# Row sums of a 16384 x 1024 matrix: 200 columns of the last row loaded by two loads over 104 and 24 partitions

## The chip, the cores and the metric

The kernel runs on one core of a Trainium2 chip. The metric is the device time of one execution in microseconds (us); smaller is better. A profile is one execution recorded by the hardware profiler.

## The reference

The input `x` has shape 32 x 512 x 1024 in float32 (67.1 MB), the output 32 x 512. Each output is the sum of 1024 numbers:

```
def reference(x):
    return np.sum(x, axis=-1).astype(np.float32)
```

There is one addition for each number read, so the work is mostly the reading of 67 MB.

## The kernel before

The 32 x 512 = 16384 rows are laid out as 8 groups of 128 partitions x 16 rows (`BIG` = 16): partition p of group g holds 16 consecutive rows, and every row is 4 KB. All loads are issued by SP (SyncE) on one DMA queue, so they are worked off in the order in which they are issued. Sums collect in one tile `sums` of 128 x 128.

The order of the loads is written out by hand. First come 7 rows per partition of the last group (`FIRST` = 7, a load that is moved to the program's entry). Then come the seven other groups whole, 16 rows per partition each, in tiles `t` with three buffers. The rest of the last group follows: six rows, two rows, and at last one row, row 15 of each partition. That last row comes in two pieces of columns, `pieces = (536, 488)`: the first piece is the load at L222, the second the load at L223. L180 issues all the loads before. Each load has 128 partitions.

Sums are made in three ways. `vec` (L141) is a reduction on DVE (VectorE) over up to 16 rows. `halves` (L155) is an operation on DVE that adds the two halves of a row and accumulates the sum; it is followed by a read of the accumulator. `act` (L168) is an activation on ACT (ScalarE) with an accumulator. The last whole group and the rows behind it are split between `halves` on DVE and `act` on ACT.

For the last row, `halves` first works on the first piece (268 pairs of numbers) and writes the sum into a column of the tile right ahead of the second piece. A zero stands behind the second piece (a memset at L220), which makes it 490 numbers. The second call of `halves` (245 pairs) sums this, so the first piece's sum is added in along the way. Its result goes to the last column of `sums`.

Two stores (L191) write the output: one on ACT's queue with the first seven groups (56 KB), which is held until the load of two rows has landed and waits for the sums, and one on SP's queue with the last group (8 KB) behind the last `halves`. At the program's end the clearing of the semaphores on POOL waits for this store.

Of the kernel before, what the change touches and what calls it, by code (L numbers as in the profile page):

```python
# [101 lines left out]
def kernel(  # L102
# [5 lines left out]
    nc = tc.nc  # L108
# [14 lines left out]
    def rows_from(j, n):  # L123
        return x_g[j // BIG, :, j % BIG : j % BIG + n, :]
# [3 lines left out]
    last = J // BIG - 1  # L128
    FIRST = 7
    pieces = (536, 488)  # L130

    with (
        tc.tile_pool(name="in", bufs=3) as inpool,
        tc.tile_pool(name="unread", bufs=4, space=bass.MemoryType.PSUM) as upool,
        tc.tile_pool(name="stage", bufs=1) as stpool,
        tc.manual_schedule(),
    ):
        sums = stpool.tile([P, J], fp32)

        def vec(dst, src):  # L140
            return nc.vector.tensor_reduce(  # L141
                out=dst, in_=src, axis=mybir.AxisListType.X, op=mybir.AluOpType.add
            )

        def hold(inst, until, reason):
            tc.add_manual_dep(
                inst.ins,
                until.ins.name,
                mybir.DependencyInfo(mybir.DependencyClass.Sync, mybir.DependencyReason.DATA),
                reason=reason,  # L150
            )

        def halves(dst, src):
            n = src.shape[-1] // 2
            return nc.vector.tensor_tensor_reduce(  # L155
                out=src[:, :n],
                in0=src[:, :n],
                in1=src[:, n:],
                scale=1.0,
                scalar=0.0,  # L160
                op0=mybir.AluOpType.add,
                op1=mybir.AluOpType.add,
                accum_out=dst,
            )

        def act(dst, src, n):
            unread = upool.tile([P, dim], fp32)
            nc.scalar.activation(  # L168
                out=unread[:, :n],
                in_=src,  # L170
                func=mybir.ActivationFunctionType.Copy,
                accum_out=dst,
            )

        sums_of = []

        def rows(t, a, n, j, n_act, pairs=False):
            nv = n - n_act
            block = t[:, a * dim : (a + n) * dim].rearrange("p (n d) -> p n d", d=dim)
            load = nc.sync.dma_start(out=block, in_=rows_from(j, n))  # L180
            if pairs:
                for q in range(nv):
                    sums_of.append(halves(sums[:, j + q : j + q + 1], block[:, q, :]))
            else:
                sums_of.append(vec(sums[:, j : j + nv], block[:, :nv, :]))
            for q in range(nv, n):
                act(sums[:, j + q : j + q + 1], block[:, q, :], dim)
            return load

        def store(eng, g0, g1):  # L190
            return eng.dma_start(  # L191
                out=out_v[:, g0:g1],
                in_=sums[:, g0 * BIG : g1 * BIG].rearrange("p (g j) -> p g j", j=BIG),
            )


        j = last * BIG
        t = inpool.tile([P, BIG * dim + 4], fp32)
        rows(t, 0, FIRST, j, 0)
        first = sums_of[-1]  # L200
        for g in range(last):
            t = inpool.tile([P, BIG * dim + 4], fp32)
            if g < last - 1:
                load = rows(t, 0, BIG, g * BIG, 0)
            else:
                rows(t, 0, BIG, g * BIG, 7, pairs=True)
            if g == 1:
                hold(load, first, "no descriptors of later loads while the first ones start")

        t = inpool.tile([P, BIG * dim + 4], fp32)  # L210
        rows(t, FIRST, 6, j + FIRST, 2, pairs=True)
        two = rows(t, FIRST + 6, 2, j + FIRST + 6, 1, pairs=True)
        a = BIG - 1

        j += a
        c, width = pieces
        whole = t[:, a * dim + c : BIG * dim + 2]
        nc.vector.memset(whole[:, width + 1 :], 0.0)  # L220
        part = t[:, a * dim : a * dim + c]
        nc.sync.dma_start(out=part, in_=rows_from(j, 1)[:, 0, :c])  # L222
        nc.sync.dma_start(out=whole[:, 1 : width + 1], in_=rows_from(j, 1)[:, 0, c:])  # L223
        hold(store(nc.scalar, 0, last), two, "its packets come behind those of the loads")
        halves(whole[:, :1], part)
        halves(sums[:, j : j + 1], whole)
        store(nc.sync, last, last + 1)
# [30 lines left out]
```

## Time and profile before

| What | us |
|---|---|
| median of three runs | 161.61 |
| the three runs | 161.74, 161.48, 161.61 |
| span of the profiled execution | 160.3 |
| the profiled execution's own time | not among the times shown |
| DVE busy | 120.6 (75% of the span) |
| ACT busy | 11.9 (7%) |
| HBM read | 67.11 MB, with writes 419 GB/s over the span |
| SP issues the load at L222, at L223 | at 126.15, at 126.65 |
| these loads, from issue to landing | 31.4 each |
| last store on SP, from issue to landing | 1.4 |

The span runs from the first to the last recorded instruction; the run's time has some work around it besides. "Landing" is the moment at which a load's semaphore has its last increment; a load that is split over 16 DMA engines gets 16 of them, each from a small closing packet on one engine. Instructions named DVEq or SPq are on the sequencer of the engine, which handles waits and DMA issues. A DMA share of 1.00 in a stretch means that on average all 16 DMA engines were busy; it can read a little over 1, since records of neighbouring packets overlap.

### The profile page before, as it was taken

To read this page: it belongs to the slowest core of one execution; us is meant where nothing else is said; L and a number is where in the kernel's file an instruction comes from. 1 tells how busy PE (TensorE), PEld (TensorE's weight loads), DVE (VectorE), ACT (ScalarE), POOL (GpSimd) and SP (SyncE) were. 2 spreads that over 40 slices of the span, in tenths; PEclk is the share of its full clock that TensorE was granted. 3 is DMA by queue.
4 is the path that set the end of the run, shared out by engine and by line. 5 is a ranking of instruction groups with operands and counts; after the bars stand their busy time and mean duration, and the time that the engine had idled before them with its cause. 6 is when DMAs were issued, how large, how long until landed. Compare 5 with 4: busy or idle time off the path is not lost.

```text
span 160.3 us, 132 instructions
## 1 busy us (share of the span) xinstructions
DVE 120.6 (75%) x40; ACT 11.9 (7%) x21; POOL 0.2 (0%) x4
## 2 busy tenths in 40 slices
DVE  0029600499986999679995999949999499994955
ACT  3000000000000000000000000000000000003993
POOL 0000000000000000000000000000000000000000
DMA  8999999899799699699699699796996996996994
GB/s 300 386 491 523 392 392 523 376 409 523 327 458 523 294 491 523 262 523 523 262 523 523 262 523 441 343 523 278 507 523 262 523 523 262 523 523 264 423 384 123
DMA packets 2784, 67.18 MB, mean 419 GB/s; under 512 B 1248, under 2 KB 1376, under 8 KB 1504
## 3 DMA queue, kind: packets, MB, share of 16 engines
q1 hardware_dynamic: 1872, 67.12, 97.7%
q10 hardware_dynamic: 912, 0.06, 0.4%
HBM read 67.11 MB, written 0.07 MB: 419 GB/s over the span
## 4 chain that ended last, share of the span: by engine, by line
DMA 71%; DVE 27%; SPq 1%; issue 0%; DVEq 0%
DMA t<-in_x_dram 71%; DVE sums L141 26%; SPq L180 0%; SPq L222 0%; DVE t L155 0%; DVEq L253 0%
## 5 line engine op out<-in xcount | busy, mean ns | idle before, releaser
L141 DVE TENSOR_REDUCE sums<-t 128x16 f32<-128x16384 f32 (+1 forms) x7 | 110.9, 15848 | 33.8 <-DMA t<-in_x_dram 33.8
L168 ACT ACTIVATE unread<-t 128x1024 f32<-128x1024 f32 x10 | 10.1, 1012 | 145.3 <-DMA t<-in_x_dram 145.3
L155 DVE CUSTOM_DVE_ANT_0 t<-t 128x512 f32<-128x512 f32 (+2 forms) x16 | 9.6, 656 | 4.1 <-DMA t<-in_x_dram 4.0
L168 ACT ACTIVATION_READ_ACCUMULATOR unread<-t 128x1 f32 x10 | 1.9, 187 | 0.0
L168 ACT ACT_TABLE_LOAD x1 | 1.3, 1283 | 0.8 <-PEq L242 0.8
L155 DVE DVE_READ_ACCUMULATOR2_ANT sums<- 128x1 f32 x15 | 1.3, 84 | 0.0
L242 POOL MEMSET const-bfloat16-1.0<- 128x1 bf16 x1 | 0.1, 101 | 0.0
L242 POOL MEMSET const-uint8-127<- 128x1 uint8 x1 | 0.1, 101 | 0.0
L242 POOL MEMSET const-float32-0.0<- 128x1 f32 x1 | 0.1, 98 | 0.2 <-issue 0.2
L242 POOL MEMSET const-float32-1.0<- 128x1 f32 x1 | 0.1, 98 | 0.0
L155 DVE DVE_READ_ACCUMULATOR2_ANT t<- 128x1 f32 x1 | 0.1, 83 | 0.0
L220 DVE MEMSET t<- 128x1 f32 x1 | 0.1, 59 | 0.0
## 6 DMA issues: line engine op xcount, KB each, us to landing
t<-in_x_dram SPq DMA_DIRECT2D x1, 3584.0 KB, 11.0
t<-in_x_dram SPq DMA_DIRECT2D x1, 3072.0 KB, 29.0
t<-in_x_dram SPq DMA_DIRECT2D x1, 1024.0 KB, 31.1
t<-in_x_dram SPq DMA_DIRECT2D x1, 268.0 KB, 31.4
t<-in_x_dram SPq DMA_DIRECT2D x1, 244.0 KB, 31.4
t<-in_x_dram SPq DMA_DIRECT2D x7, 41.1
out_dram<-sums ACTq DMA_DIRECT2D x1, 56.0 KB, 2.1
out_dram<-sums SPq DMA_DIRECT2D x1, 8.0 KB, 1.4
```

The lines of the kernel that those rows point to most:

```text
L141: return nc.vector.tensor_reduce(out=dst, in_=src, axis=mybir.AxisListType.X, op=mybir.AluOpType.add)
L155: return nc.vector.tensor_tensor_reduce(out=src[:, :n], in0=src[:, :n], in1=src[:, n:], scale=1.0, scalar=0.0, op0=mybir.AluOpType.add, op ...
L168: nc.scalar.activation(out=unread[:, :n], in_=src, func=mybir.ActivationFunctionType.Copy, accum_out=dst,)
L220: nc.vector.memset(whole[:, width + 1 :], 0.0)
L242: nc = _bacc.Bacc("TRN2", target_bir_lowering=False, num_devices=1)
```

## The change

The first piece of the last row (536 columns, 268 KB) was one load over 128 partitions. Now its first 336 columns (`EVEN`) are one load over 128 partitions (1344 bytes a partition). The other 200 columns (800 bytes a partition) come in two loads, one over partitions 0 to 103 (`FEW` = 104) and one over partitions 104 to 127. The second piece, 488 columns, is loaded after them as before. All are issued by SP, in this order. The operation on the first piece waits for three loads instead of one; the same bytes land in the same places, and the computation is the same.

```
+    EVEN = 336
+    FEW = 104
...
-        nc.sync.dma_start(out=part, in_=rows_from(j, 1)[:, 0, :c])
+        src = rows_from(j, 1)[:, 0, :]
+        nc.sync.dma_start(out=part[:, :EVEN], in_=src[:, :EVEN])
+        nc.sync.dma_start(out=part[:FEW, EVEN:], in_=src[:FEW, EVEN:c])
+        nc.sync.dma_start(out=part[FEW:, EVEN:], in_=src[FEW:, EVEN:c])
         nc.sync.dma_start(out=whole[:, 1 : width + 1], in_=rows_from(j, 1)[:, 0, c:])
```

The kernel has two DMA issues more on SP. By the order of the instructions, the eight semaphores that the DMAs take in turn are dealt out differently behind the new loads: the last `halves` waits on another one, the two stores use and wait for others, SP's last store has one wait more, and the wait of the clear on POOL follows the store. Nothing else is moved; DVE, ACT, POOL and PE have the same instructions in the same order, at line numbers two to five higher.

## The prediction

> **What bounds the kernel now.** I read the chain of waits in order of time first, then the last 2 us by instruction, then the DMA share in tenths of a microsecond, then the queue rows. The profiled execution has a span of 160.3 us. The times shown are 161.48, 161.61 and 161.74 us; the execution behind the profile has no time of its own there, so I put the 1.3 us between its span and the median around it, unchanged. My sum is a difference on that span, added to 161.61. About 0.2% (0.32 us) is what a measurement of this kernel can tell from no change.
>
> The chain's last pieces (start, length, what):
>
> ```profile
> 126.10 0.05 issue
> 126.15 0.45 SPq L222
> 126.60 0.04 issue
> 126.65 31.45 DMA t<-in_x_dram
> 158.09 0.04 issue
> 158.13 0.42 DVE t L155
> 158.54 0.01 DVEq L253
> ```
>
> The end hangs on the landing of the very last load (L223, 488 columns) at 158.09. It was issued at 126.65 and spent 31 us behind earlier loads: the queue is full, and issuing is early. Behind it come one DVE operation and the small store. How close DVE is behind shows the timeline of its last operations (start, length, engine, line):
>
> ```profile
> 157.46 0.08 DVE L155 DVE_READ_ACCUMULATOR2_ANT sums<- 128x1 f32 x1
> 157.49 0.06 DVE L220 MEMSET t<- 128x1 f32 x1
> 157.54 0.44 DVE L155 CUSTOM_DVE_ANT_0 t<-t 128x268 f32<-128x268 f32 x1
> 157.90 0.08 DVE L155 DVE_READ_ACCUMULATOR2_ANT t<- 128x1 f32 x1
> 158.13 0.42 DVE L155 CUSTOM_DVE_ANT_0 t<-t 128x245 f32<-128x245 f32 x1
> 158.47 0.08 DVE L155 DVE_READ_ACCUMULATOR2_ANT sums<- 128x1 f32 x1
> ```
>
> The operation on the first piece (268 pairs) starts at 157.54, without idle time behind DVE's own work. The accumulator read behind it ends at 157.98, and DVE's wait for that read is met at about 158.04 (the 21 ns semaphore row of L155 at 158.0). So DVE stands ready only 0.05 us before the last load lands. An earlier landing is worth 0.05 us and no more; a later one costs in full.
>
> How the 16 DMA engines run out (stretch, DVE, ACT and POOL busy, clock, mean busy share of the 16, GB/s):
>
> ```profile
> 157.10:157.20 0.10, 0.10 (x1) 0.10 (x1) 0.00 (x0) 1.00 1.20 468
> 157.20:157.30 0.10, 0.10 (x1) 0.10 (x1) 0.00 (x0) 1.00 0.72 273
> 157.30:157.40 0.10, 0.10 (x1) 0.10 (x1) 0.00 (x0) 1.00 0.49 176
> 157.40:157.50 0.10, 0.10 (x3) 0.10 (x1) 0.00 (x0) 1.00 0.41 156
> 157.50:157.60 0.10, 0.10 (x4) 0.10 (x1) 0.00 (x0) 1.00 0.11 39
> 157.60:157.70 0.10, 0.10 (x1) 0.10 (x1) 0.00 (x0) 1.00 0.06 20
> 157.80:157.90 0.10, 0.10 (x1) 0.10 (x2) 0.00 (x0) 1.00 0.07 8
> 157.90:158.00 0.10, 0.08 (x2) 0.09 (x1) 0.00 (x0) 1.00 0.91 87
> ```
>
> The engines don't finish together. By the closing packets in the trace's records eleven end by 157.40; the other five at 157.50, 157.56, 157.57, 157.64 and 157.69. The last one's closing packet is seen 0.40 us later (158.09). The kernel therefore waits for one engine out of 16, and shifting rows from late engines to early ones can in principle help. Whose numbers the late ones bear, the records don't tell. (What starts at 157.87 is the 56 KB store of ACT.)
>
> **The change, step by step.** It cuts 200 of the 536 columns of the first piece off into two loads, of 104 and 24 rows.
>
> *Issuing.* Two more issues on SP ahead of the last load, at 0.45 us (L222) or 0.44 (L223) and 0.05 between: it is issued 0.98 us later, at 127.6 instead of 126.65. Its packets start at about 156.6 at the earliest, 29 us later. The cost is nothing; without that cover it would be 0.98 us. Behind it on SP waits only the last store, for DVE.
>
> *Packets.* The queue row is
>
> ```profile
> q1 hardware_dynamic: 1872, 67.12, 97.7%
> ```
>
> SP's queue ran 12 loads and one store; 1872 / 13 = 144, that is 128 rows and 16 closing packets each: every load has eight rows on each of 16 engines. In the packet records a row of 2144 bytes takes 87 ns and one of 1952 bytes 80, so 0.0365 ns a byte (8192 bytes: 309, which fits). Packets of one engine follow each other 3 ns closer than that. By this line a row of 1344 bytes (336 columns) takes 55 ns and one of 800 bytes (200 columns) 35. Per engine, with 2 ns for each closing packet: before, 8 x 84 + 2 = 674 and 8 x 77 + 2 = 618, in sum 1292 ns (the records' own spacing). After: 8 x 55 + 2 = 442, then the rows of 200 columns, then 618. With eight such rows (282 and another closing packet) the engine needs 1344, +0.05 us; with ten 1414, +0.12; with sixteen 1624, +0.33; with none 1060, -0.23.
>
> *Who carries the rows.* No load of this trace has other than 128 rows, so the share is bounded from the nearest rows. Low end: both loads spread over all 16, eight rows an engine, +0.05. High end: eight rows an engine as in every load here, the 104 rows on 13 engines and the 24 again on three of these, sixteen rows, +0.33. I take eight and two (24 rows over the 13): ten rows, +0.12 on those engines and -0.23 on three that get none. It is nearest to the row of eight a load and needs no engine to be singled out.
>
> [...]
>
> *What this does to the end.* If the latest engine (157.69) has ten rows, it closes at 157.81 and the load lands at 158.21: +0.12. With eight rows it is +0.05. If the three latest are just the three relieved, the fourth (157.56) closes with ten rows at 157.68, -0.01; with eight it is 157.61, and the fifth with ten rows 157.62: -0.07, of which DVE lets 0.05 through. An early engine with ten rows closes by 157.52 and is never last.
>
> *The first piece.* Its operation now waits for three semaphores: one more semaphore instruction, 21 ns by the L155 row. Behind it on DVE are the accumulator read and the last operation. Its load landed at 157.52 at the latest; with +0.12 that is 157.64, so the operation starts about 0.12 later, and DVE is ready at 158.16, still before 158.21. Where the landing gains, the 21 ns eat half of DVE's 0.05. So nothing is added to a loss, and a gain is 0.03 to 0.05 at most.
>
> *Renumbered waits.* By the order of the instructions the two stores now wait on semaphores of older loads (SP's last store gets one more), which landed by 147.06; SP takes it while it waits for DVE: nothing, or 28 ns (the longest semaphore row) if it came last. ACT's store starts its packets at 157.87; loads ending by 157.81 stay ahead of it.
>
> **Sum.** Between +0.05 and +0.12 us; I take the middle, 0.09: 161.61 + 0.09 = 161.70 us.
>
> **Rivals.**
> *Relief works.* The late engines are the three without rows. For it: five engines are late by up to 0.29 us over the eleven, and three can be freed of 0.23. Against: nothing ties their places to the rows, and three relieved leave two late ones; DVE caps the gain. -0.01 to -0.05: 161.58.
> *The small rows cost double (slower).* [...] An 800-byte row at 70 ns makes ten rows 704 ns, +0.47 in all. For it: every load in the trace keeps one row pattern, so its 27 GB/s an engine (65536 bytes in 2418 ns) holds for that pattern alone. Against: it would have to last through all ten rows of a late engine. With half of the doubling +0.29: 161.90; it passes 0.32 us from about 55 ns a row, with all of it 162.08. Loads that close after 157.87 would meet ACT's store as well, at 8 ns a packet of it.
>
> [...]
> *The change doesn't spread as it says.* The 24 rows fall on three of the 13 engines with eight each: if one of them is the last, +0.33, 161.94; if an early one, 157.40 + 0.33 = 157.73, +0.04. Were all 128 rows on one engine, 128 x 35 ns = 4.5 us more, about 165.9; a load of 104 rows on one engine is against every row here.
>
> **Numbers.** Forecast (+0.05 to +0.12, the even spread included) 0.51; relief 0.25; doubled rows 0.16, of which 0.10 beyond 0.32 us; narrow shares 0.05, nearly all beyond; a gain over 0.32 us that I can't name 0.03, since DVE's cap leaves none on this path. That is faster 0.03, same 0.82, slower 0.15. The range: below, relief (161.56) less most of the 0.13 by which the runs shown scatter, 161.45; above, half-doubled rows (161.90) and 0.10 for the same scatter, 162.00.
>
> **What would show it.** The packets of q1: 2000 and one closing packet for each engine of the two new loads, so 2032 for sixteen and sixteen, 2026 for 13 and 13, 2016 with 13 and three. The closing packets of the last load: some engines near 157.0 if three carry no rows. The length of the 800-byte packets: 38 ns, or towards 70. The chain: still the last load and L157 behind it (L155 now); if the operation on the first piece takes its place, DVE has become the bound. I am wrong if the last load lands before 158.04 or after 158.3 while the loads ahead are as they were.

## The result and the profile after

The changed kernel takes 162.07 us (median of six runs, 161.91 to 162.31) against 161.55 us before (six runs, 161.43 to 161.86). The ratio is 1.003 with a 95% interval of 1.0017 to 1.0044: slower by 0.3 to 0.7 us. The forecast was 161.70 in a range of 161.45 to 162.00. The median lies above the range; the interval starts inside it (161.82 us), but above the forecast's +0.05 to +0.12.

The two first profiles have the same span, 160.3 us, and that misleads. The changed kernel's profiled execution took 162.12 us, so 1.8 us lie around its span, not 1.3; a second trace of the kernel before (below) has a span of 159.8 at 161.58, again 1.8 around it. By that measure the first trace of before was an execution of some 162.1 us. Its early loads ran late: the two-row load landed at 156.82, in the second trace at 156.31. So I count from that landing. From there to the end of the span the kernel before needs 3.50 and 3.49 us (two traces), the changed one 3.96 and 3.82. All times "after the two-row load" below are counted so.

The chain's end in the profile after (start, length, what):

```profile
126.92 30.46 DMA t<-in_x_dram
157.38 0.03 issue
157.41 0.05 DVEq L157
157.46 0.08 issue
157.54 0.46 DVE t L157 x2
158.00 0.03 issue
158.03 0.02 DVEq L157
158.05 0.09 issue
158.13 0.42 DVE t L157
158.55 0.01 DVEq L258
```

The load at the head of this chain was issued at 126.92: it is the load of 24 rows, no longer the last one. It landed at 157.38, then come a semaphore instruction (DVEq), the operation on the first piece, a second semaphore instruction and the last operation. The end now hangs on the landing of the first piece and on DVE behind it. The last load landed at 157.77, 0.36 us before the operation that needs it began. DVE's timeline shows the hole:

```profile
156.39 0.69 DVE L157 CUSTOM_DVE_ANT_0 t<-t 128x512 f32<-128x512 f32 x1
157.01 0.08 DVE L157 DVE_READ_ACCUMULATOR2_ANT sums<- 128x1 f32 x1
157.04 0.06 DVE L222 MEMSET t<- 128x1 f32 x1
157.54 0.44 DVE L157 CUSTOM_DVE_ANT_0 t<-t 128x268 f32<-128x268 f32 x1 [0.44 <-DMA t<-in_x_dram]
```

Between the memset and the operation on the first piece lie 0.44 us of idle time that ended with a DMA; before, there were none. The DMA engines in the same tail (stretch, three engines' busy time, clock, mean busy share of the 16 DMA engines, GB/s):

```profile
156.20:156.40 0.20, 0.20 (x3) 0.01 (x1) 0.00 (x0) 1.00 1.12 387
156.40:156.60 0.20, 0.20 (x1) 0.20 (x1) 0.00 (x0) 1.00 1.17 414
156.60:156.80 0.20, 0.20 (x1) 0.20 (x1) 0.00 (x0) 1.00 1.10 303
156.80:157.00 0.20, 0.20 (x1) 0.20 (x1) 0.00 (x0) 1.00 0.85 225
```

The kernel before, with its last load under way:

```profile
156.80:157.00 0.20, 0.20 (x3) 0.16 (x1) 0.00 (x0) 1.00 1.02 397
157.00:157.20 0.20, 0.20 (x1) 0.20 (x1) 0.00 (x0) 1.00 1.11 429
```

After the change, from 156.60 on, the engines are as busy as ahead of it (1.10) and move a quarter less (303 GB/s for 414; 429 at 1.11 before): the packets became longer. In the records the 800-byte packets all take 38 ns, as worked out; it is the 1952-byte packets of the last load behind them that take up to 144 ns, 97 in the mean, instead of 80. And the first piece's last landing (157.38) comes 0.81 us after the end of its last data packet (156.57); before, this lag was 0.445 us (0.455 in the second trace).

The queue's row after the change:

```profile
q1 hardware_dynamic: 2025, 67.12, 97.6%
```

2025 is 2000 + 13 + 12: the two narrow loads have 13 and 12 closing packets, and as many landings in the trace, where each load of 128 rows has 16.

### The profile page after: what moved, and what is told of

Its sections match the earlier page's. It is cut to its first block, busy times and chain, and to the rows that moved or that the text cites. A ratio compares the mean times of both kernels' runs of the same rounds, so it can differ in the third digit from the quotient of the medians.

```text
span 160.3 us, 135 instructions
## 1 busy us (share of the span) xinstructions
DVE 120.7 (75%) x40; ACT 11.9 (7%) x21; POOL 0.2 (0%) x4
## 3 DMA queue, kind: packets, MB, share of 16 engines
q1 hardware_dynamic: 2025, 67.12, 97.6%
## 4 chain that ended last, share of the span: by engine, by line
DMA 71%; DVE 27%; SPq 1%; issue 0%; DVEq 0%
DMA t<-in_x_dram 71%; DVE sums L143 26%; DVE t L157 1%; SPq L182 0%; SPq L226 0%; SPq L225 0%; DVEq L157 0%; DVEq L258 0%
```

## The experiments

Lag means: from the end of a piece's last narrow (or last) data packet to its last landing. "Packets" are those of the last load (1952 bytes, 80 ns undisturbed), mean. The last three columns are us after the two-row load's landing: start of the operation on the first piece, landing of the last load, end of the span. Lags, packets and these columns are from one trace each.

| Kernel | ratio to before (95%) | lag us | packets ns | first op | last load | end |
|---|---|---|---|---|---|---|
| before, 1st trace | | 0.45 | 80 | 0.72 | 1.28 | 3.50 |
| before_again | one run, 161.58 us | 0.46 | 80 | 0.70 | 1.27 | 3.49 |
| after, 1st trace | 1.003 (1.0017 to 1.0044) | 0.81 | 97 | 1.18 | 1.40 | 3.96 |
| after_again | 1.004 (1.0026 to 1.0054) | 0.73 | 100 | 1.03 | 1.36 | 3.82 |
| one_more_even | 1.0007 (0.9997 to 1.0017) | 0.45 | 80 | 0.86 | 1.31 | 3.64 |
| two_more_even | 1.0018 (1.0006 to 1.0029) | 0.54 | 80 | 1.00 | 1.35 | 3.77 |
| narrow_first | 1.0015 (1.0007 to 1.0024) | 0.49 | 91 | 0.85 | 1.29 | 3.62 |
| last_load_in_the_op | 1.0023 (1.0014 to 1.0031) | 0.83 | 100 | 0.98 | 1.37 | 3.77 |
| two_halves | 1.0042 (1.0026 to 1.0058) | 0.80 | 91 | 1.26 | 1.50 | 4.04 |
| narrow_400 | 1.0052 (1.004 to 1.0064) | 0.93 | 123 | 1.37 | 1.69 | 4.16 |
| spare_middle | 1.0016 (1.0006 to 1.0025) | 0.54 | 80 | 0.72 | 1.60 | 3.82 |
| spare_lower | 1.0059 (1.0044 to 1.0074) | 1.05 | 134 | 1.09 | 2.24 | 4.45 |
| spare_even | 1.0025 (1.0013 to 1.0038) | 0.58 | 84 | 0.78 | 1.70 | 3.91 |

Two theories stood at first. **A**: closing packets that follow each other closely land late, and DVE reaches the operation through a semaphore instruction. **B**: the narrow loads themselves land late and stretch the packets behind them, as the changed kernel's trace has it (0.81 us for 0.45, 97 ns for 80); why they should, no trace had shown.

**One load more, none narrow.**

```
-        nc.sync.dma_start(out=part[:FEW, EVEN:], in_=src[:FEW, EVEN:c])
-        nc.sync.dma_start(out=part[FEW:, EVEN:], in_=src[FEW:, EVEN:c])
+        nc.sync.dma_start(out=part[:, EVEN:], in_=src[:, EVEN:c])
```

> First piece in two loads of 128 partitions (336 and 200 columns), so one load more than before and no narrow one. Theory A (closing packets that follow each other closely land late, and DVE reaches the first piece's operation through a semaphore instruction): two closings 0.28 us apart; the 200-column load's last landing lags its last closing packet by 0.5 to 0.65 us instead of 0.44, the operation on the first piece starts 0.85 to 1.0 us after the two-row load has landed (before 0.72, changed kernel 1.18), time +0.15 to +0.3 us against before. [...]

No added lag (0.45) and no stretch, as B has it. The operation starts at 0.86, as A has it, but not for a late closing: 0.13 us of that lie between the landing and the operation, the price of the semaphore instruction. The time can't be told from before.

**Two loads more, none narrow.**

```
+        nc.sync.dma_start(out=part[:, EVEN:EVEN + 100], in_=src[:, EVEN:EVEN + 100])
+        nc.sync.dma_start(out=part[:, EVEN + 100:], in_=src[:, EVEN + 100:c])
```

> First piece in three loads of 128 partitions (336, 100 and 100 columns): as many loads, closings and waits as the changed kernel, every engine with eight rows of each. Theory A: closings of the three loads 0.17 us apart on every engine, last landing of the first piece lags by 0.7 us or more, packets of the last load stretched over 80 ns, time +0.4 to +0.55 us against before, as the changed kernel. [...]

Here A loses: with as many loads, closings and waits as the changed kernel, the lag is 0.54 and not 0.81, and no packet is stretched. The time is +0.1 to +0.5 us. The end comes 0.27 us later than before, so part of the changed kernel's loss comes from the number of loads and the wait.

**The narrow loads first.** The two narrow loads are issued ahead of the one with 336 columns.

> The changed kernel's four loads with the two narrow ones ahead of the 336-column load. Theory A: the closings of the narrow loads have 0.44 us of data behind them before the 336-column load closes; its landing lags by 0.45 to 0.55 us, the operation on the first piece starts 0.85 to 1.0 us after the two-row load has landed (changed kernel 1.18), time +0.1 to +0.3 us against before. [...]

The narrow loads lag as ever (the 24 rows land 0.84 us after their last packet), but the load behind them, which now closes the piece, lags only 0.49, while its packets stretch from 58 to at most 115 ns. Time (+0.1 to +0.4 us) fits A's number. Most of the added lag is gone by the landing of the 336 columns (an estimated 0.44 us of reading by the prediction's packet prices), though packets of the last load still took up to 144 ns.

**The late load in the operation's own wait.**

```
+            if isinstance(inst, mybir.InstCustomDveAnt) and len(inst.sync_info.on_wait) == 3:
+                waits = sorted(inst.sync_info.on_wait, key=lambda w: w.ant_name, reverse=True)
```

> The changed kernel with the order of the three waits turned round: the semaphore instruction ahead of the operation holds the two earlier loads, the operation itself the last one (24 rows). If DVE and its wait are the bound, the operation starts 0.03 to 0.05 us after the landing instead of 0.16, time 0.1 us less than the changed kernel (+0.35 to +0.45 us against before). If the last load is the bound, no difference from the changed kernel (+0.5 us).

The chain's end in this run:

```profile
126.87 30.63 DMA t<-in_x_dram
157.49 0.02 issue
157.52 0.46 DVE t L161 x2
```

The operation now starts 0.02 us after the landing instead of 0.16: 0.14 us are the wait through the semaphore instruction. The ratio of 1.0023 against 1.003 and 1.004 points the same way, though the intervals overlap; the trace is the better witness.

**The changed kernel again, equal halves, twice the columns, and before again** came next. For the halves `FEW` is 64, for the columns `EVEN` is 136.

> The changed kernel once more, for its time beside the others on one chip and for a second trace of it. Time +0.35 to +0.6 us against before. By what the runs before this one showed: the last landing of the first piece lags its last 800-byte packet by 0.75 to 0.85 us, the operation on the first piece starts 0.14 to 0.17 us after that landing, and the end comes 3.9 to 4.0 us after the landing of the two-row load.

> The changed kernel with the 200 columns cut after partition 63 instead of 103: both loads have 64 partitions, every engine should have four rows of each, and as many as in the kernel with three even loads. [...] Theory C (what costs is the unequal share of the engines, ten rows on some, and engines left out): shares are equal, so the lag is 0.45 to 0.55 us as in the even loads, packets stay at 80 ns, time +0.2 to +0.3 us as with three even loads.

> The changed kernel with 400 columns instead of 200 in the two narrow loads (136 in the first load). [...] Theory C or a fixed price of a load with fewer engines: the lag stays at 0.75 to 0.85 us; ten rows of 1600 bytes put 0.06 us more than ten of 800 on the engines, time +0.5 to +0.65 us.

> The kernel before once more, for a second trace of it. If the 160.3 us of the first trace were an execution whose early loads were slow, the span here is 159.7 to 160.1 us, with the end 3.45 to 3.55 us after the landing of the two-row load as in the first trace; if the time outside the span differs between the two kernels instead, the span is 160.2 to 160.4 us again at a time of 161.6.

The second trace of the changed kernel has the same 0.16 us between landing and operation, a lag of 0.73, just under what was expected, and an end at 3.82, ahead of the 3.9 to 4.0 expected: two traces of one kernel differ by 0.14 us there. With equal halves both loads have 16 closing packets (2032 in the queue's row), so no engine is left out and, if the rows are spread evenly, each has eight; the piece lags by 0.80 all the same, where three even loads lagged by 0.54: it isn't the unequal shares (theory C). Twice the columns give a lag of 0.93 for 0.81 and 0.73, and its own packets are stretched too: those of 1600 bytes take up to 136 ns instead of 67, and the last load lands 0.3 us later than in the changed kernel. The time is +0.84 us (0.65 to 1.03); C's upper end (0.65) is only just reached by the interval.

**Which partitions, first try.** Theory B in two forms: by B1 it matters which partitions a load covers, by B2 any load of fewer than 128 lags. That 32 to 95 should do better than 0 to 63 was my guess; no run before these had shown it. The first piece ends in two loads of 200 columns over the same 64 partitions; the other 64 get these 400 columns ahead of the six-row load.

```
+        nc.sync.dma_start(out=part[:, :136], in_=src[:, :136])
+        nc.sync.dma_start(out=part[32:96, 136:336], in_=src[32:96, 136:336])
+        nc.sync.dma_start(out=part[32:96, 336:536], in_=src[32:96, 336:536])
```

> Built to set beside the next run: the first piece ends in a load of 136 columns over 128 partitions and two loads of 200 columns over 64 partitions, 32 to 95 both times; the 400 columns of the other 64 partitions come early, ahead of the six-row load. [...] Theory B2 (any load with fewer than 128 partitions lags): 0.75 to 0.85 us and stretched packets, as with the two halves.

> The same as the run with rows 32 to 95, with partitions 0 to 63 in both late loads: same loads, sizes, number of packets, waits and order. [...] Theory B2: no difference between the two, within 0.05 us.

Lags of 0.64 (32 to 95) and 0.97 us (0 to 63), packets of 83 and 131 ns, one run each at 162.16 and 163.49 us. It agrees with B1, but isn't clean: the early loads differed too, and the landings of the two-row load were already spread over 0.77 and 0.98 us (0.41 before).

**Which partitions, clean.** The kernel before, with two loads more between its two pieces, into a tile that nothing reads. The operations wait for the same loads as before.

```
         nc.sync.dma_start(out=part, in_=rows_from(j, 1)[:, 0, :c])
+        nc.sync.dma_start(out=spare[32:96, 0:200], in_=src[32:96, 0:200])
+        nc.sync.dma_start(out=spare[32:96, 200:400], in_=src[32:96, 200:400])
```

The second kernel has `0:64` for `32:96`, the third `:` with columns 0 to 99 and 100 to 199.

> The kernel before with two loads more between its two pieces of the last row, into a tile that nothing reads: 200 columns over partitions 32 to 95, twice. No wait in the tail is changed, so only what the loads do to each other is seen. [...] Theory B2 (any load of fewer than 128 partitions): lag 0.75 us or more and packets stretched, as in the run with 0 to 63.

> The same with partitions 0 to 63 in both spare loads. [...] Theory B2: as with 32 to 95 within 0.05 us.

> The same bytes in two spare loads over all 128 partitions, 100 columns each (8 rows of 400 bytes an engine instead of 4 of 800). [...]

This decides for B1 against B2. The same bytes in the same packets cost 0.3 us over partitions 32 to 95 and 0.95 us over 0 to 63 (1.0016 and 1.0059 of 161.63). With 0 to 63 the lag is 1.05 us for 0.54, and the last load lands 0.64 us later. The tail with 32 to 95, then the one with 0 to 63 (columns as above):

```profile
156.60:156.80 0.20, 0.20 (x1) 0.20 (x1) 0.00 (x0) 1.00 1.14 420
156.80:157.00 0.20, 0.20 (x2) 0.20 (x1) 0.00 (x0) 1.00 1.05 404
157.00:157.20 0.20, 0.20 (x4) 0.20 (x1) 0.00 (x0) 1.00 0.82 312
157.20:157.40 0.20, 0.20 (x1) 0.20 (x2) 0.00 (x0) 1.00 0.25 88
```

```profile
156.60:156.80 0.20, 0.20 (x1) 0.20 (x1) 0.00 (x0) 1.00 1.25 336
156.80:157.00 0.20, 0.20 (x2) 0.20 (x1) 0.00 (x0) 1.00 1.07 215
157.00:157.20 0.20, 0.08 (x3) 0.20 (x1) 0.00 (x0) 1.00 1.34 254
157.20:157.40 0.20, 0.00 (x0) 0.20 (x2) 0.00 (x0) 1.00 0.82 146
```

At 156.80 both tails have their DMA engines busy all the time (1.05 and 1.07), but the first moves 404 GB/s and the second 215, about half. A load of 64 rows isn't slow as such here: with 32 to 95 lag and packets (0.54 us, 80 ns) are those of the even loads (0.58, 84). It is slow over 0 to 63 (1.05, 134), so what counted in these runs is which partitions it covers, or which rows in HBM: these go with the partitions, and the runs can't tell the two apart. Nor do they show why 0 to 63 are the slow ones. That the 104 and 24 rows of the changed kernel lag for the same reason is inferred from the same signs (a long lag, longer packets behind, and the two halves, which lag too); no run moved those rows alone to other partitions.

**Relief without the tail.** The kernel before, with the last 200 numbers that each partition gets of the last whole group (the end of its 16th row) in loads over 104 and 24 partitions.

```
+                e = n * dim - 200
+                nc.sync.dma_start(out=flat[:104, e:], in_=src[:104, e:])
+                nc.sync.dma_start(out=flat[104:, e:], in_=src[104:, e:])
+                load = nc.sync.dma_start(out=flat[:, :e], in_=src[:, :e])
```

> The kernel before, with the last 200 columns of the last whole group's 16 rows (instead of the last row's) in two loads over 104 and 24 partitions, some 30 us ahead of the end: the three engines without narrow rows read 6.4 KB less each, and neither the backlog nor the waits fall into the tail. If the late engines are those three, the 16 landings of the two-row load lie closer together (0.40 to 0.59 us from first to last so far; 0.25 to 0.35 us here), the end still comes 3.45 to 3.55 us after the last of them, and time is 0.03 to 0.1 us less than before (ratio 0.9994 to 0.9998, within what can be told from none). If they aren't, the landings spread over 0.5 to 0.7 us and time is +0.05 to +0.15 us.

The 16 landings of a load, 0.60 us apart from first to last just ahead of the narrow loads, were 0.37 apart behind them, and the end came 3.47 us after the two-row load. That agrees with relief, but doesn't show it alone: in spare_middle the landings went from 0.54 to 0.37 us apart far ahead of its narrow loads. The tails say more. In the four traces with 104 and 24 rows of 200 columns in the tail, the last load's landings are 0.21 to 0.35 us apart, the two-row load's 0.41 to 0.59; with one or two even loads more they stay at 0.50 (0.52) and 0.46 (0.53). So the late engines are most likely those without narrow rows. Yet the time is 1.0021 of before (1.0008 to 1.0034), slower. Why isn't shown; the profiled execution was one of the shorter ones (161.73, the runs 161.69 to 162.66). No version here beats the kernel before.

## Why the prediction was wrong

*Issuing, packet prices and shares: right.* The issues took 0.36 to 0.47 us some 29 us ahead. Packets of 58 and 38 ns are what the line through the old ones gave; the narrow loads have 13 and 12 closing packets, from which the ten, eight and no rows of the sum follow if the rows are spread evenly and the 12 engines are among the 13; the records don't show that engine by engine.

*"If the latest engine has ten rows": wrong in its condition.* In the changed kernel the last 336-column packet ends at 156.35 and the last 800-byte packet at 156.57, 0.22 us later; ten rows need 0.35. So the engine that was latest had not ten narrow rows, and the last load's landings, closer together than the two-row load's (0.34 us for 0.49), agree. Reading without stretch would have ended at 156.57 + 0.62 = 157.19, 0.82 us after the two-row load (0.87 before); stretched packets made it 0.95. The last load's landing, 1.40 and 1.36 instead of 1.28, so came to the forecast's +0.05 to +0.12 by luck, on another road: relief, and a stretch that more than ate it.

*"DVE is ready at 158.04, 0.05 us before the last load": wrong.* From the start of the semaphore instruction to the operation behind it 0.105 us pass, in the trace of before (158.02 to 158.13) and in that of after (158.03 to 158.13), where the load had long landed. DVE had no time to spare. I took the 21 ns of the instruction for the cost of the wait.

*"The first piece … its load landed at 157.52; with +0.12 that is 157.64": the step that failed.* It moved the landing by reading time alone and kept the lag of 0.44 us. Against before, the operation on the first piece starts 0.45 us later in the first trace (1.18 for 0.72), and the end follows it: 0.46. Of the 0.45, 0.31 us are the later landing (1.01 for 0.70) and 0.14 the wait through the semaphore instruction, counted as 21 ns. The last packet of the piece ended even earlier than before (0.20 us after the two-row load for 0.26), so the whole of the later landing is lag, 0.81 for 0.45. In the second trace the operation starts 0.31 to 0.34 us later than before (1.03), 0.17 to 0.20 of it the landing and 0.14 the wait.

*The rival "small rows cost double"* laid the cost on the narrow loads, where the runs show it, and its +0.35 us for ten rows is near the lag that was added (0.37 and 0.27 in the two traces). That its 162.08 lies beside the measured 162.07 is luck: 0.14 us of the loss is a wait that it didn't have. It had the wrong place and too small a chance. I looked for 70 ns in the narrow packets; in the changed kernel's trace all 128 stay at 38, so that term isn't shown, and the cost shows in landings (0.81 us for 0.45) and in packets behind (97 ns for 80). And I laid it on the last load, which landed only 0.12 and 0.08 us later, instead of on the first piece, which closes right behind the narrow rows and on which DVE waits.

*The rival "relief works"* was most likely right on the late engines in these traces, and worth nothing, since DVE was the bound already.

*The 1.3 us around the span* moved no term of the sum, but hid that the first trace was a slow sample of the early loads.

How much of the 0.5 us is due to what: two_more_even, which has the loads and the wait but nothing narrow, costs 0.18%, the changed kernel 0.3 to 0.4%. By the traces the end comes 0.27 us later with two_more_even and 0.33 to 0.46 with the changed kernel. So about half or more belongs to the loads and the wait, the rest to the narrow loads; the intervals allow no closer split.

## What to carry to other kernels

Here the changed kernel's narrow loads, each over part of the partitions, showed their packets unstretched (38 ns for 800 bytes) and still landed late (a lag of 0.81 us for 0.45); take a load's price from the lag between its last packet and its landing, and try it over other partitions (0.54 us over 32 to 95, 1.05 over 0 to 63). Where two paths end together, a piece's readiness counts as much as the last load's landing, so cost each one's wait: a wait that an instruction holds itself took 0.02 to 0.04 us here, one in a semaphore instruction ahead of it 0.13 to 0.16. Compare two traces from a common event near the change, since equal spans can come of unlike executions.

## What the runs showed that I had not expected

With spare loads over partitions 0 to 63, even the full load ahead of them landed late: 0.81 us after its own last packet, which ended at 156.61, against 0.46 us with 32 to 95. Only the loads issued behind it differed, so here later loads went with a landing 0.35 us later of an earlier one.

SP's issue of a load of 64 partitions took 0.53 to 0.59 us, against 0.43 to 0.48 for most of the tail's loads of 128; in the kernels with spare narrow loads and with halves the load of 128 right behind them took 0.58 to 0.59 too. Some 30 us ahead of their use, it cost nothing.
